# Two of four late transposes evicted on ScalarE, and one output half finished by an adding transfer

## The chip, the cores and the metric

The kernel runs on one core of one Trainium2 chip. The metric is the device time of one execution in microseconds, and the number compared is the median over several executions. Two of the core's engines matter beside TensorE (PE): VectorE (DVE) and ScalarE (ACT), which both read what PE leaves in PSUM and write SBUF. GpSimd (POOL) computes small reciprocal roots and issues the adding transfers, SyncE (SP) issues all the other transfers.

## The reference, cut to what matters

One layer of a decoder trunk, over a prompt of 1024 positions and 8 single samples, all in float32 with D = 1024:

```
xn   = rmsnorm(x, pre_g)
u, v, z_a, x_b, z_b, g_a, g_b = split(xn @ w_in)            # seven blocks of 1024 columns
y_a  = gelu(u) * spatial_mix(layernorm(gelu(v))) * silu(z_a)
y_b  = pooled(x_b) * silu(z_b)
m    = sigmoid(g_a) * (y_a @ w_pa) + sigmoid(g_b) * (y_b @ w_pb)
h    = x + rmsnorm(m @ w_out, post_g)
gate = sigmoid(rmsnorm(h, ple_in_g) @ w_pg)
y    = h + rmsnorm(gate * (p @ w_ple), ple_out_g)           # the main output
```

The change touches the start (xn is transposed, so that features lie on partitions) and the last line (the sum with h, for one half of one tile of 128 positions).

## The kernel before, in words

Tokens are cut into 8 tiles of 128 (`t` = 0 to 7) and the 8 samples (`t` = S). Every large product is one level of Strassen: seven half-size products P1 to P7. Each half-size product is three passes over the high and low parts of its operands (a float32r copy from ACT, the remainder from DVE; `split`, line 432).

**The order of the work** is not that of the code. All operations are first recorded, then a planner (class `Planner`, line 100) runs a list schedule over them with costs of its own, and writes out one fixed order for each engine. It computes for each operation a due time backwards from its readers (`late`, line 249), lets an operation start only a fixed lead ahead of that (14.98 us for a load that takes a fresh slot, 14.0 us for others; line 291), and among those that could start now takes the one with the earliest due time (line 305). It is written for `SLOTS` = 46 buffers in SBUF and for PSUM regions that it hands on in turn: three two-bank regions ("acc") and two single banks ("bank"). On the chip each engine and each queue runs its list in order and waits on semaphores.

**The start.** `begin` (line 1729) loads x, normalises it and transposes it on PE. `x_half(j, kps)` (line 965) does one half of the tokens: for each pair `kp` of feature blocks it transposes four x tiles into a PSUM region (`kp` 0, 2, 3) or two banks (`kp` 1), eight transposes in all, and evicts the pair with two instructions of 128x512 that also multiply by the norm's gain. `SIDES[4 * j + kp]` (lines 29 and 979) says by which engine: 1 is ACT, 0 is DVE. The first half (`j` = 0) is done early. The second (`j` = 1, "late") comes after the first four products, in the order of `SCRIPT` (line 36): `kp` 0 and 1, then 2 and 3, then the cut of its blocks into high and low parts.

**The end.** The last product group works on tiles 6 and 7, with its seven products in the order `LAST` (line 1622): P4 closes the first half of tile 7, P3 the second half of tile 6, and P3 is run in two column parts of 256 (`run_halves`, line 779). For each part that is ready, `gated` (line 1566) takes the sigmoid on ACT, multiplies by e on DVE, sums the squares on ACT and multiplies by the output gain on DVE. `gate_finish(t)` (line 1575) then takes the reciprocal root of the sum (one small add on DVE, one power on POOL). Tiles 0 to 5 then multiply by root and gain and have h added by a transfer of POOL that reads h from DRAM and adds it into SBUF, after which SP writes the tile out. Tiles 6, 7 and the samples load h into a slot `hback` ahead of time, and for each half of 512 columns one DVE instruction does gate times root plus h, and SP writes the half out.

Of the kernel before, what the change touches and what calls it, by code (L numbers as in the profile page):

```python
# [11 lines left out]
AF = mybir.ActivationFunctionType  # L12
ALU = mybir.AluOpType
# [3 lines left out]
NB = D // P  # L17
# [3 lines left out]
HALF = 512  # L21
# [4 lines left out]
EPS = 1e-6  # L26
POOL_BUF = 15
FAST = (1, 1, 0, 1)
SIDES = (0, 1, 0, 0, 0, 1, 0, 0)
EARLY = 40.0  # L30
WE = 1
PUSH = {'hs': -4.0, 'norm': -5.0, 'half': 0.0, 'cut': -1.0, 'e': 2.0, 'we': -2.0, 'vw': -9.0, 'p': 3.0}
# [349 lines left out]
def hybrid_step(  # L382
# [7 lines left out]
    nc = tc.nc  # L390
# [15 lines left out]
    def slot(name, shape=(P, T), dt=F32):  # L406
        n_name[0] += 1
        name, n = f"{name}_{n_name[0]}", 1
        for d in shape[1:]:
            n *= d  # L410
        model = big.rearrange("p b t -> p (b t)")[:, :n].bitcast(dt)
        if len(shape) > 2:
            dims = "abc"[: len(shape) - 1]
            model = model.rearrange(f"p ({' '.join(dims)}) -> p {' '.join(dims)}", **dict(zip(dims, shape[1:])))
        return plan.slot(name, model, lambda i: spool.tile(list(shape), dt, tag=f"slot{i}", name=name, bufs=1))
# [21 lines left out]
    def dma(out, in_, by=None):  # L437
        (by or nc.sync).dma_start(out=out, in_=in_)
# [20 lines left out]
    nc = plan  # L459
# [13 lines left out]
    def rstd(parts, n=P, r=None):  # L473

        t, r = sm("ms"), sm("rstd") if r is None else r
        nc.vector.tensor_scalar(out=t[:n], in0=parts[-1][:n], scalar1=EPS if len(parts) == 1 else parts[0][:n],
                                scalar2=None, op0=ALU.add)
        nc.gpsimd.tensor_tensor(out=r[:n], in0=t[:n], in1=mhalf[:n], op=ALU.pow)
        return r
# [312 lines left out]
    class User:  # L792

        func = AF.Copy
# [170 lines left out]
    def x_half(j, kps):  # L965

        for kp in kps:
# [9 lines left out]
            for kk in range(2):  # L977
                o, i, gain = out[:, kk], ps[kk], col(0, 2 * kp + kk)
                if SIDES[4 * j + kp]:
                    nc.scalar.activation(out=o, in_=i, func=AF.Copy, scale=gain)  # L980
# [36 lines left out]
    class V(User):  # L1017

        func = AF.Gelu_apprx_tanh
# [158 lines left out]
    class Gate(User):  # L1178
        func = AF.Sigmoid
# [7 lines left out]
    class U(User):  # L1187
        func = AF.Gelu_apprx_tanh
# [4 lines left out]
    class ZA(User):  # L1193
        func = AF.Silu
# [84 lines left out]
    class ZB(User):  # L1279
        func = AF.Silu  # L1280
# [174 lines left out]
    y_of = lambda t: y_sample if t == S else y_prompt[t * P : (t + 1) * P, :]  # L1455
# [119 lines left out]
    def gate_finish(t):  # L1575
        r = rows(t)
        rs = rstd(parts.pop(t), r)
        g = ge.pop(t)
        del e_of[t]
        if t < NB - 2:  # L1580
            nc.vector.scalar_tensor_tensor(out=g, in0=g, scalar=rs, in1=gains["out"],
                                           op0=ALU.mult, op1=ALU.mult)
            nc.gpsimd.dma_start(out=g, in_=kept["h"][t * P : (t + 1) * P, :], accum_op=ALU.add)
            dma(y_of(t), g)
            return
        h = slot("hback", (P, D))
        dma(h[:r], kept["h"][t * P : t * P + r, :])
        for j in range(2):
            nc.vector.scalar_tensor_tensor(out=g[:r, half(j)], in0=g[:r, half(j)], scalar=rs[:r],
                                           in1=h[:r, half(j)], op0=ALU.mult, op1=ALU.add)  # L1590
            dma(y_of(t)[:, half(j)], g[:r, half(j)])

    class Embed(User):
# [7 lines left out]
        def summed(self, m, j, ps, u, free=None):  # L1601
            t = 2 * self.pair + m
            o = ge[t][:, half(j)]
            add(o, ps, u)
            gated(t, half(j), o)
            if j == 0:
                gate_finish(t)
        def finish(self):
            for m in range(2):
                if 2 * self.pair + m in ge:  # L1610
                    gate_finish(2 * self.pair + m)

    def embed_gate_sample(ps):
        ge_start(S)
        o = slot("sgate", (P, D))
        sample_sums(ps, o)
        for j in range(2):
            gated(S, half(j), o[:NS, half(j)])
        gate_finish(S)
# [242 lines left out]
```

## Time and profile before

| | |
|---|---|
| median of three runs | 978.81 us (977.58 to 979.65) |
| the profiled execution's own time | 977.26 us |
| its span, first to last instruction | 975.6 us |
| PE busy | 963.1 us (99%) |
| DVE busy | 813.4 us (83%) |
| ACT busy | 497.9 us (51%) |
| POOL busy | 74.2 us (8%) |
| granted TensorE clock, mean over the span | 0.998 |

The profiled execution is one execution; 1.7 us of its time lie outside its span. It ran 1.55 us below the median of the three timed runs.

### The profile page before, as it was taken

Reading aid. Unit: us, or ns where it says so; the run is one execution under the profiler, and the core shown is the slowest. Engines: PE = TensorE matmul, PEld = TensorE weight load, DVE = VectorE, ACT = ScalarE, POOL = GpSimd, SP = SyncE. Lnnn points to the kernel's source line nnn. Section 1 sums busy time; section 2 is a strip of 40 time slices with the busy share of each in tenths; the row PEclk is TensorE's granted clock in tenths of the full one; section 3 lists DMA queues with packets and bytes.
Section 4 is the critical chain, followed back from the end, with each engine's and each line's share of the span. In section 5 each row is a group of like instructions: output and inputs, shape, how many; then the busy total and the mean of one; then the engine's idle time right before and its main releaser. Section 6 shows DMA issues by size and latency. Waiting matters only on the chain. (4 is left out here: it accounts for less than half of the span.)

```text
span 975.6 us, 15918 instructions
## 1 busy us (share of the span) xinstructions
PE 963.1 (99%) x6037; PEld 855.9 (88%) x6037; DVE 813.4 (83%) x1261; ACT 497.9 (51%) x852; POOL 74.2 (8%) x117
## 2 busy tenths in 40 slices
PE   8999999999999999999999999999999999999996
PEld 6789899999999999999999999999999997788775
DVE  6998568988889788868698897698699899779987
ACT  7664345766444443242434343563263274698655
POOL 2200000000000000000010100000000001323212
PEclk9999999999999999999999999999999999999999
DMA  9523955423467464453425366692492385799896
GB/s 327 172 105 68 192 124 183 155 97 119 164 226 261 136 203 160 140 195 120 152 99 183 134 214 238 228 384 89 158 382 92 111 301 189 151 299 313 224 320 215
DMA packets 128506, 185.82 MB, mean 190 GB/s; under 512 B 42150, under 2 KB 85198, under 8 KB 128421
## 3 DMA queue, kind: packets, MB, share of 16 engines
q1 hardware_dynamic: 126381, 177.43, 54.9%
q0 software_dynamic: 2048, 7.37, 4.1%
q8 instruction: 47, 0.77, 0.3%
q14 instruction: 30, 0.25, 0.1%
HBM read 129.27 MB, written 55.96 MB: 190 GB/s over the span
## 5 line engine op out<-in xcount | busy, mean ns | idle before, releaser
L374 DVE TENSOR_TENSOR u<-acc,u 128x520 f32<-128x520 f32 (+1 forms) x89 | 62.0, 696 | 35.5 <-PE acc L374 35.2
L374 POOL TENSOR_TENSOR rstd<-ms,mhalf 128x1 f32<-128x1 f32 (+1 forms) x37 | 30.9, 841 | 520.3 <-DVE ms L374 517.7
L374 ACT ACTIVATE u<-acc 128x512 f32<-128x512 f32 (+1 forms) x43 | 25.6, 596 | 44.2 <-PE acc L374 44.0
L374 DVE TENSOR_TENSOR big<-big 128x1024 f32<-128x1024 f32 (+4 forms) x20 | 23.8, 1219 | 0.0
L374 POOL COPY big<-xb 128x1 f32<-128x1 f32 x8 | 3.4, 419 | 260.4 <-ACT xb L374 219.7
L374 ACT ACTIVATE paw<-pas 128x512 fp32r<-128x512 f32 x16 | 10.0, 630 | 24.0 <-DVE pas L374 18.2
L374 ACT ACTIVATE pbw<-pbs 128x512 fp32r<-128x512 f32 x16 | 10.0, 628 | 22.1 <-DVE pbs L374 16.8
L374 PE MATMUL accm<-qh,wpoolw 128*128 128x260 f32 (+1 forms) x96 | 20.9, 319 | 0.0
L374 ACT ACTIVATE big<-mix 128x256 f32<-128x256 f32 x32 | 12.0, 382 | 17.1 <-PE mix L374 16.4
L374 ACT ACTIVATE gbw<-gbs 128x512 fp32r<-128x512 f32 x16 | 10.1, 630 | 19.3 <-DVE gbs L374 10.0
L374 DVE SCALAR_TENSOR_TENSOR zb<-accm,gvec,zb 128x512 f32<-128x512 f32 (+1 forms) x16 | 12.0, 754 | 9.4 <-PE accm L374 9.2
L374 ACT ACTIVATE zaw<-zas 128x512 fp32r<-128x512 f32 x16 | 10.0, 628 | 18.1 <-DVE zas L374 10.0
L374 ACT ACTIVATE junk<-h 128x512 bf16<-128x512 f32 x25 | 15.7, 628 | 3.4 <-DVE h L374 2.9
L374 PEld LDWEIGHTS accm<-qh,wpoolw 128*128 128x128 f32 x96 | 15.6, 188 | 1.9
L374 ACT ACTIVATE zbw<-zbs 128x512 fp32r<-128x512 f32 x16 | 10.1, 628 | 13.8 <-DVE zbs L374 8.2
L374 ACT ACTIVATE u<-acct 128x512 f32<-128x512 f32 x22 | 13.0, 589 | 7.4 <-PE acct L374 4.6
L374 DVE TENSOR_TENSOR paw<-pas,paw 128x512 fp32r<-128x512 f32 x16 | 10.9, 688 | 6.7 <-ACT paw L374 6.7
L374 ACT ACTIVATE mw<-ms 128x512 fp32r<-128x512 f32 x16 | 10.0, 625 | 12.4 <-DVE ms L374 9.7
L374 ACT ACT_TABLE_LOAD x11 | 14.1, 1283 | 4.0 <-PE acc L374 2.3
L374 ACT ACTIVATE zbw<-zbraw 128x512 fp32r<-128x512 f32 x12 | 7.5, 623 | 16.6 <-DMA zbraw<-in_w_in_dram 10.7
L374 ACT ACTIVATE gbw<-gbraw 128x512 fp32r<-128x512 f32 x12 | 7.4, 624 | 16.4 <-DMA gbraw<-in_w_in_dram 14.3
L374 PE MATMUL mix<-wst,vh 128*128 128x256 f32 x64 | 15.5, 320 | 0.0
(655 smaller groups left out, 3560.5 us busy)
## 6 DMA issues: line engine op xcount, KB each, us to landing
ga<-ga SPq DMA_DIRECT2D x16, 516.0 KB, 4.6
gb<-gb SPq DMA_DIRECT2D x16, 516.0 KB, 6.2
ya<-za SPq DMA_DIRECT2D x8, 516.0 KB, 3.6
yb<-zb SPq DMA_DIRECT2D x8, 516.0 KB, 4.5
x<-in_x_prompt_dram SPq DMA_DIRECT2D x8, 512.0 KB, 9.3
vraw<-in_w_in_dram SPq DMA_DIRECT2D x8, 512.0 KB, 6.4
e<-e SPq DMA_DIRECT2D x8, 512.0 KB, 3.6
vturned<-v SPq DMA_DIRECT2D x32, 128.0 KB, 4.5
```

What stands on the lines that cost most here:

```text
L374: getattr(getattr(self.nc, e), method)(*(self.real(a) for a in args), **{k: self.real(a) for k, a in kwargs.items()})
```

## The change

Two edits. The table `SIDES` gives the late pairs `kp` 0 and 2 to ACT, where before it gave `kp` 1 alone; `kp` 1 goes back to DVE. And for tile 6 (the seventh) the second half is finished otherwise: SP copies the second half of h from its slot to the output; ACT multiplies the gate by the root in place; POOL issues a transfer from SBUF to the output in DRAM that adds. The first half of tile 6, tile 7 and the samples stay as they were.

```diff
-SIDES = (0, 1, 0, 0, 0, 1, 0, 0)
+SIDES = (0, 1, 0, 0, 1, 0, 1, 0)
...
         h = slot("hback", (P, D))
         dma(h[:r], kept["h"][t * P : t * P + r, :])
+        if t == NB - 2:
+            dma(y_of(t)[:, HALF:], h[:, HALF:])
         for j in range(2):
+            if t == NB - 2 and j:
+                nc.scalar.activation(out=g[:, HALF:], in_=g[:, HALF:], func=AF.Copy, scale=rs)
+                nc.gpsimd.dma_start(out=y_of(t)[:, HALF:], in_=g[:, HALF:], accum_op=ALU.add)
+                continue
             nc.vector.scalar_tensor_tensor(out=g[:r, half(j)], in0=g[:r, half(j)], scalar=rs[:r],
                                            in1=h[:r, half(j)], op0=ALU.mult, op1=ALU.add)
             dma(y_of(t)[:, half(j)], g[:r, half(j)])
```

## Rows read from the trace of the kernel before

**Rows 1.** The page: span, and busy time of the two busiest engines.

```profile
span 975.6 us, 15918 instructions
PE 963.1 (99%) x6037; PEld 855.9 (88%) x6037; DVE 813.4 (83%) x1261; ACT 497.9 (51%) x852; POOL 74.2 (8%) x117
```

**Rows 2.** Busy time by stage: us, then each engine; clock, transfers' share, GB/s.

```profile
41.00:911.00 870.00, 870.00 (x5582) 784.43 (x5582) 728.50 (x1110) 430.11 (x718) 47.77 (x56) 1.00 0.56 180
...
967.60:975.60 8.00, 0.00 (x0) 0.00 (x0) 4.51 (x10) 1.36 (x5) 1.53 (x2) 0.72 0.59 231
```

**Rows 3.** PE in order of time around the late transposes; idle time in brackets.

```profile
35.96 2.78 PE L374 MATMUL pst<-ident,x 128*128 128x128 f32 x24
39.46 1.06 PE L374 MATMUL pst<-ident,x 128*128 128x128 f32 x8 [0.72 <-DVE big L374]
40.78 0.47 PE L374 MATMUL acc<-xB11h,vw 128*128 128x512 f32 x1 [0.25 <-DVE big L374]
```

**Rows 4.** PE in order of time, the last part of P3.

```profile
966.20 0.39 PE L374 MATMUL acct<-wgB22h,hw 128*128 128x256 f32 x1 [0.56 <-ACT ge L374]
```

**Rows 5.** DVE in order of time in the same stretch as rows 3.

```profile
37.91 4.07 DVE L374 TENSOR_SCALAR big<-pst,gvec 128x512 f32<-128x512 f32 x6 [0.21 <-PE pst L374]
```

**Rows 6.** ACT in order of time in the same stretch.

```profile
37.73 0.63 ACT L374 ACTIVATE vw<-vs 128x512 fp32r<-128x512 f32 x1 [0.97 <-DVE vs L374]
38.27 1.25 ACT L374 ACTIVATE big<-pst,gvec 128x512 f32<-128x512 f32 x2
40.67 1.07 ACT L374 ACTIVATE xB22h<-big 128x1040 fp32r<-128x1040 f32 x1 [1.15 <-DVE big L374]
```

**Rows 7.** POOL in order of time: the last reciprocal root, tile 6's.

```profile
969.89 0.66 POOL L374 TENSOR_TENSOR rstd<-ms,mhalf 128x1 f32<-128x1 f32 x1 [1.43 <-DVE ms L374]
```

**Rows 8.** DVE in order of time: its last two instructions, tile 6's two halves.

```profile
970.73 1.41 DVE L374 SCALAR_TENSOR_TENSOR ge<-ge,rstd,hback 128x512 f32<-128x512 f32 x2
```

**Rows 9.** ACT in order of time: an instruction of 128x512 on SBUF.

```profile
966.49 0.63 ACT L374 ACTIVATE junk<-ge 128x512 bf16<-128x512 f32 x1 [0.34 <-DVE ge L374]
```

**Rows 10.** SP in order of time: the issues of tile 6's two halves.

```profile
971.50 0.33 SPq L374 DMA_DIRECT2D out_dram<-ge  x1
972.16 0.33 SPq L374 DMA_DIRECT2D out_dram<-ge  x1
```

**Rows 11.** The tile out_dram from 969 on: issue to landing of the last outputs.

```profile
L374 SPq DMA_DIRECT2D out_dram<-ge x4: 332/332/333, 969.7 to 972.2; - x4
...
DMA to landing us min/median/max: 2.1/2.1/2.1
```

**Rows 12.** The tile h, 903 to 905: one adding transfer, 512 KB, DRAM to SBUF.

```profile
L374 POOL DMA_DIRECT2D h<-in_x_prompt_dram x1: 879/879/879, 904.0 to 904.0; - x1
...
DMA to landing us min/median/max: 5.3/5.3/5.3
```

**Rows 13.** The tile ge, 955 to 957.2: the last but one adding transfer, 512 KB.

```profile
L374 POOL DMA_DIRECT2D ge<-h x1: 894/894/894, 956.5 to 956.5; - x1
...
DMA to landing us min/median/max: 5.7/5.7/5.7
```

**Rows 14.** Transfer queues: packets, MB, share of 16 engines; 959 to 961, then 970.4 to 971.3.

```profile
q0 software_dynamic: 92, 0.38, 95.1%
...
q1 hardware_dynamic: 139, 0.26, 76.1%
```

**Rows 15.** The tile hback: its loads, and issue to landing of the last.

```profile
L374 SPq DMA_DIRECT2D hback<-h x3: 291/319/492, 948.4 to 958.7; - x3
...
DMA to landing us min/median/max: 9.6/9.6/9.6
```

**Rows 16.** Busy time by stage near the end, columns as in rows 2.

```profile
962.00:966.00 4.00, 3.64 (x24) 3.08 (x22) 4.00 (x9) 2.25 (x6) 0.15 (x1) 1.00 1.00 275
966.00:969.50 3.50, 1.34 (x9) 1.14 (x9) 2.96 (x8) 2.25 (x8) 0.93 (x1) 1.00 1.00 403
969.50:972.00 2.50, 0.00 (x0) 0.00 (x0) 2.50 (x6) 0.00 (x0) 0.66 (x1) 0.81 0.45 175
```

## The prediction

> **What bounds the kernel now.** I read the busy totals first: PE is busy for 963.1 of 975.6 us, DVE for 813.4 and ACT for half [rows 1]. A total is an average, so next the table by stage: from 41 to 911 us PE is busy for 870.00 of 870.00 us [rows 2]. No edit to DVE or ACT work in that stretch can shorten it; it could only open a hole in it. What PE loses lies at the two ends. So I went to PE in order of time and looked for its brackets. Around the late transposes it stands still twice, 0.72 us before the last pair is transposed and 0.25 us before the next product, both times because DVE has not yet emptied PSUM [rows 3]; near the end it waits 0.56 us for ACT between the two parts of P3 [rows 4]. Last, the stage behind PE's last instruction: 8.0 us from 967.6 to the end in which PE does nothing and the time is a chain of small steps [rows 2]. Both edits lie in these places: the first can touch the 0.72 and 0.25 us, the second the last 8 us. Together they can't give much, and the question is the sign.
>
> **Part 1, the late transposes.** Before, DVE empties pairs 0, 2 and 3, six instructions in 4.07 us (0.68 us from one to the next), beginning when PE has transposed the last x tile at 37.91 us [rows 5]; ACT empties pair 1, two in 1.25 us (0.62 each) [rows 6]. Pair 3 needs the region of pair 0, and PE restarts at 39.46, which is 37.91 + two DVE instructions + a handover of about 0.15 us [rows 3, 5]. The product at 40.78 waits for the region of pair 2, the fourth DVE instruction [rows 3, 5].
>
> After, ACT has pairs 0 and 2, DVE pairs 1 and 3. No instruction is added or removed, two change places: DVE loses 1.36 us of work in a stage where it is the late one, ACT gains 1.25 us in one where it idled 1.15 us straight afterwards [rows 6]. ACT is free when pair 0 is ready, if the weight split that stands at 37.73 [rows 6] goes behind the evictions. It should: the planner ranks by due time, and pair 0's region is wanted by the next transposes at once, while that split feeds a later product. Then: ACT takes pair 0 at 37.91 and is through at 39.16 (1.25 us), PE restarts at about 39.31 instead of 39.46; pair 3's transposes (1.06 us) end at 40.37; ACT takes pair 2 from 39.16 to 40.41, so the product can start near 40.50 instead of 40.78. Gain about 0.3 us, and since PE is solid from there to 911 us [rows 2], it is carried to the end of PE's work. The bounds: if the split stays in front, ACT starts pair 0 at 38.27 [rows 6], and the restart comes at 39.67, 0.2 us later than before; if both holes closed, 0.97 us would be won [rows 3], which the transposes of pair 3 in series with an eviction don't allow. I take −0.3. What hides the rest: the cut of the second half, 1.07 us on ACT at 40.67 [rows 6], begins when pair 2 is out, and that comes no later than before.
>
> **Part 2, the end.** Before, tile 6's root leaves POOL at 969.89 + 0.66 = 970.55 [rows 7]. DVE is still busy with tile 7 and does tile 6's halves as its last two instructions from 970.73 to 972.14 [rows 8]. SP issues them at 971.50 and 972.16 [rows 10], and 2.1 us after the last issue the transfer has landed [rows 11]: 974.26. The remaining 1.3 us of the span is the program's close and stays.
>
> Removed: one DVE instruction (0.70 us, half of rows 8) and the last SP issue. With nothing in their place the last landing would be that of the first half, 971.50 + 2.1 = 973.6, a gain of 0.65 us.
>
> Added, on the path: ACT's product, 0.63 us by an instruction of the same size [rows 9], from 970.6, when the root is there, to 971.25 (ACT has little else there: 1.36 us of work in those last 8 us [rows 2]). Then POOL issues the adding transfer at about 971.3. Nothing is queued behind it on POOL. That is 0.86 us ahead of the old last issue. But the transfer is of another kind. The trace has adding transfers of 512 KB alone, from DRAM into SBUF: 5.3 us from issue to landing [rows 12], 5.7 us with a second one beside it [rows 13]. None of 256 KB and none into DRAM is shown. In the stretch with only the adding queue at work, 92 packets of 4 KB took 95.1% of 16 engines for 2.0 us, so 0.33 us each [rows 14]; 128 rows over 16 engines are 8 packets in turn, 2.65 us. Rows half as long, at the same rate per byte, save 1.3 us: 5.3 − 1.3 = 4.0 us. Bounds: 2.1 us if it is no dearer than a plain write of the same bytes [rows 11], 5.7 us if the cost goes by packets and not by bytes [rows 13]. I take 4.0, since it is made of the nearest rows. Landing 971.3 + 4.0 = 975.3, against 974.26 before: +1.05 us. With the bounds, from 973.6 (the first half is then last, −0.65) to 977.0 (+2.75).
>
> The Trainium skill, page "DMA: Bandwidth & Descriptors", section "Anatomy of one DMA — SWDGE (gpsimd) path", fits such a transfer as about 2.0 us plus bytes over 436 thousand per us, so an estimate of 2.6 us for 256 KB and 3.2 us for 512 KB. By it the transfer would land at 973.9, 0.35 us ahead of before, and the median would be some 978.2 us. For 512 KB this trace shows 5.3 us [rows 12] and not 3.2, so here the measurement decides.
>
> Added, off the path: SP copies the second half of h to the output, one issue of about 0.33 us [rows 10] and 256 KB. By rows 14 a plain 256 KB (some 128 packets of 2 KB at 76.1% of 16 engines in 0.9 us) is about 0.7 us of all engines. It falls into a stage in which the engines are full, 1.00 from 962 to 969.5 [rows 16], and pushes the outputs of tiles 4 and 5 back by 0.7 us; from 969.5 to 972 the share is 0.45 [rows 16], which takes that up before the last transfers. It adds two waits. SP waits for the load of h before it can issue the copy, and behind it in SP's order stand the samples' and the tiles' outputs; POOL waits for the copy's landing. The last load of h takes 9.6 us from its issue at 958.7, until 968.3 [rows 15], because the adding transfers hold the engines. I expect the load to move up, as it now has a reader with an earlier due time (the planner adds issue and transfer of the copy, some 3 us against 0.8 us for the DVE instruction), so the copy is out before 968 and this costs nothing. If the cover fails, it is the second rival.
>
> **The sum.** −0.3 + 1.05 = +0.75 us on the profiled execution: 977.26 to 978.0. That execution was 1.55 us below the median of the runs shown, so the forecast for the median is 978.81 + 0.8 = 979.6 us. What a measurement of this kernel can tell from no change is 0.2%, here 1.96 us: 976.85 to 980.77.
>
> **Rivals.**
> 1. *The adding transfer costs by the packet.* For: there are 128 rows either way, and an adding packet of 4 KB took 0.33 us, four times the 0.08 us of a plain one of 2 KB (76.1% of 16 engines, 0.9 us, 139 packets), so more than bytes is in it [rows 14]. Against: the plain 2 KB packets are so short that a floor per packet is not in sight. It decides if a 2 KB adding packet takes as long as the 0.33 us of a 4 KB one. Then 5.7 us, landing 977.0: +2.75 − 0.3 = +2.45, 981.3 us, slower.
> 2. *The copy of h blocks SP.* If the planner leaves the load where it is and puts the copy ahead of the outputs, SP stands until 968.3. Then 256 KB of h, two outputs of 512 KB, three of 256 KB and the adding transfer of 1.3 us follow in one stream: 0.7 + 2 × 1.3 + 3 × 0.7 + 1.3 = 6.7 us from the first packet at about 969.1, so 975.8, and with some 0.2 us to the landing 976.0: +1.75 − 0.3, 980.3 us. For: the 9.6 us [rows 15]; against: the earlier due time.
> 3. *The adding transfer is cheap.* If it is hardly dearer than a plain write of the same bytes, 2.1 to 2.5 us, it lands by 973.8 and the end is that of DVE's half or just behind: −0.45 to −0.65, with −0.3: 978.0 us. For: the engines are not full by then [rows 16]. Against: 5.3 us in rows 12. The Trainium skill's fit above is of this kind.
> 4. *The new order opens a hole in the middle.* All planned work behind 38 us is put in order anew, with other buffers. For: 870 us without a hole [rows 2] leave only one direction. Against: ACT is busy for half of that stretch, DVE for 84%, so there is slack. 1.5 to 3 us: 982 us.
> 5. *The first edit does nothing*, as the order on ACT keeps the split in front: +0.2 instead of −0.3, 980.1 us.
>
> **How the numbers follow.** Forecast (978.9 to 980.4) 47%, rival 1 16%, rival 2 8%, rival 3 16%, rival 4 6%, rival 5 7%. The range holds 8 in 10 if it reaches from rival 3 to rival 1 with the scatter of a median (the three runs lie within 2 us): 977.6 to 981.7. Slower by over 0.2%: most of rival 1, rival 4, and the upper edge of rival 2: 0.20. Faster by over 0.2% needs 1.96 us, but the holes and the gain at the end add up to 0.97 + 0.65 = 1.6 us at the very best: 0.04, for scatter. Within: 0.76.
>
> **What would show it.** In the profile after: PE's brackets at 39 to 41 us sum to about 0.65 us instead of 0.97; ACT has four evictions of 128x512 there, ahead of the split; PE's last instruction comes about 0.3 us earlier; DVE ends with one instruction for tile 6; an ACT instruction of 0.63 us follows POOL's root, and POOL's issue comes near 971 us; its landing is 4.0 us later and ends the span. Wrong would be: an adding transfer of under 3 us or over 5, SP idle from 963 to 968 us ahead of the copy, or a bracket of PE between 41 and 911 us.

## The result, and the profile after

The changed kernel takes 980.28 us (median of 17 runs, 978.52 to 984.65), the kernel before 978.84 us (17 runs, 976.88 to 980.66): ratio over all runs 1.0020, 95% interval [1.0012, 1.0028], so 1.2 to 2.7 us slower (the two medians alone give 1.0015). The forecast was 0.8 us slower, 979.6. The profiled execution of after took 981.77 us, with a span of 980.1; it lies 1.5 us above its median, and that of before 1.55 us below its own, so of the 4.5 us between the two spans a good part is not the change.

First the page of after, to be held against [rows 1]:

```profile
span 980.1 us, 15910 instructions
PE 965.2 (98%) x6037; PEld 856.7 (87%) x6037; DVE 811.0 (83%) x1258; ACT 499.7 (51%) x855; POOL 75.4 (8%) x118
```

PE is busy for 2.1 us longer with the same 6037 matmuls. That hints that something beside waits has changed, but it is only a hint: run 2 below, in which PE's pace is that of before, also has 964.9 us. Next PE in order of time around the late transposes, against [rows 3] (start, duration, operation, idle time in brackets):

```profile
36.51 3.44 PE L374 MATMUL pst<-ident,x 128*128 128x128 f32 x30
39.77 1.18 PE L374 MATMUL acc<-xB11h,vw 128*128 128x512 f32 x4
40.80 0.38 PE L374 MATMUL pst<-ident,x 128*128 128x128 f32 x2
40.93 0.71 PE L374 MATMUL acc<-xB11l,vw 128*128 128x512 f32 x2
...
42.41 0.39 PE L374 MATMUL e<-wehi,ph 128*128 128x512 f32 x1
```

No bracket is left: both holes are gone, 30 of the 32 transposes follow one another, and four matmuls of the next product go ahead of the last two. The last of these rows is the first product with the next weights; in the trace of before, in the same view, it is

```profile
43.18 0.39 PE L374 MATMUL e<-wehi,ph 128*128 128x512 f32 x1
```

The same stretch on ACT, against [rows 6]:

```profile
36.71 0.60 ACT L374 ACTIVATE v<-acc 128x512 f32<-128x512 f32 x1 [1.25 <-PE acc L374]
38.45 2.42 ACT L374 ACTIVATE big<-pst,gvec 128x512 f32<-128x512 f32 x4 [1.15 <-PE pst L374]
40.91 1.07 ACT L374 ACTIVATE xB22h<-big 128x1040 fp32r<-128x1040 f32 x1
41.89 1.14 ACT L374 ACTIVATE vw<-vs 128x512 fp32r<-128x512 f32 x2
```

and on DVE, against [rows 5]:

```profile
38.56 1.41 DVE L374 TENSOR_SCALAR big<-pst,gvec 128x512 f32<-128x512 f32 x2 [0.34 <-PE pst L374]
39.89 0.68 DVE L374 TENSOR_TENSOR vs<-vraw,vraw 128x512 f32<-128x512 f32 x1
40.60 0.69 DVE L374 TENSOR_TENSOR vs<-vs,vraw 128x512 f32<-128x512 f32 x1
41.21 1.41 DVE L374 TENSOR_SCALAR big<-pst,gvec 128x512 f32<-128x512 f32 x2
```

The product before the transposes is emptied first (`v<-acc`), then come four evictions on ACT, the weight split behind them, and two pairs of instructions on DVE with room between. Then what PE waited for in the rest of the span; the view's columns are who waits for whom, us in total, times and the longest:

```profile
PE acct L374 <- ACT ge L374: 1.0, 1, 1.0
PE acct L374 <- ACT u L374: 1.0, 2, 0.5
```

The first is the wait inside P3, 0.56 us before [rows 4] and 0.6 in every run below, so the 1.0 is this execution's own; the second, two waits at 873 and 893 us, is not in the trace of before. Last the end, against [rows 7 to 11]: POOL, ACT and DVE in order of time, then the last two issues and the time from issue to landing (least, median, most).

```profile
972.78 0.66 POOL L374 TENSOR_TENSOR rstd<-ms,mhalf 128x1 f32<-128x1 f32 x1 [1.25 <-DVE ms L374]
974.61 0.92 POOL L374 DMA_DIRECT2D out_dram<-ge  x1 [1.17 <-ACT ge L374]
```

```profile
973.48 0.72 ACT L374 ACTIVATE ge<-ge,rstd 128x512 f32<-128x512 f32 x1 [1.39 <-POOL rstd L374]
```

```profile
972.95 1.41 DVE L374 SCALAR_TENSOR_TENSOR ge<-ge,rstd,hback 128x512 f32<-128x512 f32 x2
```

```profile
L374 SPq DMA_DIRECT2D out_dram<-ge x1: 333/333/333, 974.4 to 974.4; - x1
L374 POOL DMA_DIRECT2D out_dram<-ge x1: 923/923/923, 974.6 to 974.6; - x1
...
DMA to landing us min/median/max: 2.2/3.1/4.1
```

The root is out at 972.78 + 0.66 = 973.44; ACT is through at 974.20; POOL issues 0.41 us later, at 974.61; and of the two transfers SP's plain one takes 2.2 us and POOL's adding one 4.1, so the adding one ends the work at 974.61 + 4.1 = 978.7. From the root to that landing it is 5.3 us; before it was 974.26 − 970.55 = 3.7 [rows 7, 10, 11].

### The profile page after: what moved, and what is told of

The parts are those of the page before. It is cut to its first block, busy times and chain, and to the rows that moved or that the text cites. A ratio compares the mean times of both kernels' runs of the same rounds, so it can differ in the third digit from the quotient of the medians.

```text
span 980.1 us, 15910 instructions
## 1 busy us (share of the span) xinstructions
PE 965.2 (98%) x6037; PEld 856.7 (87%) x6037; DVE 811.0 (83%) x1258; ACT 499.7 (51%) x855; POOL 75.4 (8%) x118
## 5 line engine op out<-in xcount | busy, mean ns | idle before, releaser
L374 ACT ACTIVATE uw<-us 128x512 fp32r<-128x512 f32 x16 | 10.0, 626 | 12.5 <-DVE us L374 11.0
```

Of the source, the lines that this page charges most:

```text
L374: getattr(getattr(self.nc, e), method)(*(self.real(a) for a in args), **{k: self.real(a) for k, a in kwargs.items()})
```

## The experiments

Twelve kernels were run. The first four share a chip and one set of runs of before, the next four another, then three and one; each ratio is against its own set.

**1. The first edit alone.**

```diff
-SIDES = (0, 1, 0, 0, 0, 1, 0, 0)
+SIDES = (0, 1, 0, 0, 1, 0, 1, 0)
```

> The first edit alone; the end is as before. Theory (the loss is the adding transfer at the end, the first edit wins a little): PE's two brackets of 0.72 and 0.25 us at 39 to 41 us are gone, PE's last instruction comes 0.5 to 1.3 us earlier than in the kernel before, root to last landing stays 3.7 us, and the median is 0.3 to 1.3 us below before (ratio 0.9987 to 0.9997). Rival (the new order of all planned work costs something between 41 us and the end): PE's end no earlier, brackets of PE at 870 to 900 us as in the kernel after, median 0 to 1 us above before.

Measured: 978.75 us, ratio 0.9999 [0.9990, 1.0008]. Both holes at 39 to 41 us are closed as in after, yet the time is that of before. The gain is made and lost again. Neither expectation held whole: the median isn't below before, and of the rival's brackets at 870 to 900 us there is one, of 0.26 us.

**2. The second edit alone** (`SIDES` as before, the six added lines of `gate_finish` kept).

> The second edit alone; the late transposes are as before. Theory: root to last landing 5.2 us as in the kernel after instead of 3.7, PE's brackets at 39 to 41 us stay 0.97 us, median 1.5 to 2.0 us above before (ratio 1.0015 to 1.002). Rival (the new order costs): root to landing still 5.2, but the median is no more than 1.0 us above before, with the rest of the loss of 1.4 us coming with the first edit.

Measured: 980.27 us, ratio 1.0018 [1.0010, 1.0027]: the whole loss. POOL in order of time, and the landings from 971.4 us on:

```profile
971.47 0.66 POOL L374 TENSOR_TENSOR rstd<-ms,mhalf 128x1 f32<-128x1 f32 x1 [1.43 <-DVE ms L374]
973.29 0.92 POOL L374 DMA_DIRECT2D out_dram<-ge  x1 [1.16 <-ACT ge L374]
```

```profile
DMA to landing us min/median/max: 2.0/3.0/3.9
```

From the root (972.13) to the landing (973.29 + 3.9 = 977.2) it is 5.1 us.

**3. After, with POOL's last transfer a plain write** (that half is then without h).

```diff
-                nc.gpsimd.dma_start(out=y_of(t)[:, HALF:], in_=g[:, HALF:], accum_op=ALU.add)
+                nc.gpsimd.dma_start(out=y_of(t)[:, HALF:], in_=g[:, HALF:])
```

> The kernel after, but POOL's last transfer writes instead of adding, so h is left out of the second half of tile 6. It prices the adding by itself: same queue, same bytes, same waits. Theory (the adding is dear): issue to landing falls from 4.07 us to about 2.6 us, the median by about 1.3 us against the kernel after, to within 0.3 us of before. Rival (what is dear is a transfer from POOL's queue, whatever it does): issue to landing stays above 3.6 us and the median changes by under 0.5 us.

Measured: 978.33 us, ratio 1.0000 [0.9991, 1.0009]. The same engine, queue, bytes and place, and only the adding gone:

```profile
L374 SPq DMA_DIRECT2D out_dram<-ge x1: 333/333/333, 971.4 to 971.4; - x1
L374 POOL DMA_DIRECT2D out_dram<-ge x1: 622/622/622, 971.6 to 971.6; - x1
...
DMA to landing us min/median/max: 2.2/2.4/2.6
```

2.6 us instead of 4.1: the loss at the end is the adding. A part of it is in POOL's own issue, which took 0.62 us here and 0.92 in after (the 622 and 923 ns of the rows).

**4. After, with SP writing that half, plain** (again without h).

```diff
-                nc.gpsimd.dma_start(out=y_of(t)[:, HALF:], in_=g[:, HALF:], accum_op=ALU.add)
+                dma(y_of(t)[:, HALF:], g[:, HALF:])
```

> The kernel after, but the scaled second half of tile 6 is written by SP without adding, so h is left out there too. It prices POOL's issue and queue: against e3 only the queue differs. Theory: issue to landing 2.1 us, and the last landing is then that of DVE's first half or of this one, about 2.0 us before that of the kernel after; the median 1.5 to 2.3 us below after, 0.2 to 0.8 us below before. Rival (POOL's queue costs nothing beside SP's, the adding is all): the median within 0.3 us of e3.

Measured: 978.12 us, ratio 1.0001 [0.9992, 1.0010]. Against run 3 that is 0.2 us, which these runs can't resolve: whose queue it is costs nothing that shows. The 2.1 us from issue to landing did not come: in the trace SP's write issued at 971.88, when ACT was through, landed 2.9 us later, 3.7 us behind the root, as POOL's did in run 3.

**Where the early gain goes.** PE has no bracket from 71 to 855 us in these traces, but for one of 0.2 us in run 3, at a granted clock of 1.00, so the place to look is the time that PE takes between two fixed products. In order of time on PE, the first product of an early and of a late group, in before:

```profile
70.61 0.40 PE L374 MATMUL acc<-xT1h,vw 128*128 128x260 f32 x2
...
855.01 0.39 PE L374 MATMUL acct<-woB21h,mw 128*128 128x512 f32 x1
```

and in after:

```profile
69.92 0.40 PE L374 MATMUL acc<-xT1h,vw 128*128 128x260 f32 x2
...
855.55 0.39 PE L374 MATMUL acct<-woB21h,mw 128*128 128x512 f32 x1
```

784.40 us before, 785.63 after: the same matmuls take 1.23 us longer, in the same order but for two groups of 24 that change places at 80 to 86 us. The view by stage shows PE busy for all 784.00 us from 71 to 855 in both, at a clock of 1.00. Its counts, 5156 matmuls and 5148, are no measure of the pace: PE comes to 71 us at another place in its work, and run 5 below, which isn't slow, has 5150.

```profile
71.00:855.00 784.00, 784.00 (x5156) 713.72 (x5155) 648.77 (x995) 362.86 (x602) 30.32 (x41) 1.00 0.55 176
```

```profile
71.00:855.00 784.00, 784.00 (x5148) 713.17 (x5147) 646.50 (x992) 362.61 (x601) 30.08 (x41) 1.00 0.55 176
```

In runs 1, 3 and 4, all with the new `SIDES`, the stretch takes 785.44, 785.86 and 785.41 us; in run 2, with the old one, 784.45. So it goes with the first edit, and not with the chip, which these four runs share. What that edit changes behind 42 us, beside the order on DVE and ACT and the two groups on PE, is which tensors go into which PSUM region and which of the 46 slots. A slot is as long as the longest tensor that it holds, 4160 bytes per partition in nearly all and 4128 in one before, and they lie one behind another; a slot of 4128 moves the start of all later ones by 32 bytes against a multiple of 64. In the layout before, 4 slots begin at a multiple of 64 and 42 lie 32 past one; after, 25 and 21, since a second slot is now short. That gave a theory that could be tried without touching the order of the work.

**5. The first edit, all slots 4160 bytes long.** The slots' tensors become views of one size, here and in 6, 7 and 9 to 12; 46 slots begin at a multiple of 64. In the built programs every engine does the same in the same order as in run 1, with the same slots and PSUM regions; only the addresses in SBUF differ. The same holds for 6, 7, 9 and 10 against before, and for 11 against after.

```diff
-        return plan.slot(name, model, lambda i: spool.tile(list(shape), dt, tag=f"slot{i}", name=name, bufs=1))
+        def make(i):
+            t = spool.tile([P, 1040], F32, tag=f"slot{i}", name=name, bufs=1)[:, :n].bitcast(dt)
...
+        return plan.slot(name, model, make)
```

> The first edit alone, with every slot in SBUF 4160 bytes long, so that all slots begin at a multiple of 64 bytes; nothing in the order of the work changes against the first edit alone. Theory (PE runs slower when its operands lie in slots of which some begin at 0 and some at 32 bytes past a multiple of 64): PE keeps the 1.35 us that it is ahead at 42 us, so PE ends 0.9 to 1.5 us earlier than before, and the ratio is 0.9986 to 0.9992. Rival (the steady loss comes from the new order, or from which buffers are handed to whom): PE loses 1.0 to 1.2 us between 71 and 870 us again, and the ratio is 0.9995 to 1.0005.

Measured: 977.25 us, ratio 0.9993 [0.9984, 1.0003]. By the time alone the two theories aren't told apart (the interval holds both), but the trace does it: the stretch takes 784.26 us, and the gain is still there at 855 us.

**6. Before, all slots 4160 bytes long.**

> The kernel before, with every slot 4160 bytes long, so that all begin at a multiple of 64 bytes (before, nearly all begin 32 bytes past one). Same order. Both theories: within 0.5 us of before, ratio 0.9995 to 1.0005; the theory of the starts needs in addition that PE, measured from 42 to 870 us, takes the same time as before within 0.2 us. If PE is faster than before by over 0.5 us there, a start at a multiple of 64 is better in itself, and not only a mixture worse.

Measured: 977.13 us, ratio 0.9997 [0.9989, 1.0006]. PE in order of time:

```profile
70.79 0.40 PE L374 MATMUL acc<-xT1h,vw 128*128 128x260 f32 x2
...
854.79 0.39 PE L374 MATMUL acct<-woB21h,mw 128*128 128x512 f32 x1
```

784.00 us, 0.4 us shorter than before, a little outside what the theory allowed.

**7. Before, with the mixture put in by hand**: 21 slots at a multiple of 64, 25 at 32 past one, same order and same slots for the same tensors as in 6 (the edit is shown against 6).

```diff
-            t = spool.tile([P, 1040], F32, tag=f"slot{i}", name=name, bufs=1)[:, :n].bitcast(dt)
+            t = spool.tile([P, 1048 if i == MID else 1040], F32, tag=f"slot{i}", name=name, bufs=1)[:, :n].bitcast(dt)
```

with `MID = 20`.

> The kernel before, with the slots of the first part beginning at a multiple of 64 bytes and those behind the twentieth 32 bytes past one. Same order. Theory (mixed starts slow PE): PE takes 0.5 to 1.2 us longer than before between 71 and 870 us, spread evenly and without a bracket; ratio 1.0005 to 1.0012. Rival (the new order or the hand-out of buffers): PE takes the same time as before within 0.2 us there, ratio 0.9995 to 1.0005.

Measured: 978.80 us, ratio 1.0013 [1.0002, 1.0024]. PE in order of time (line 375 here is line 374 elsewhere):

```profile
70.55 0.41 PE L375 MATMUL acc<-xT1h,vw 128*128 128x260 f32 x2
...
856.46 0.40 PE L375 MATMUL acct<-woB21h,mw 128*128 128x512 f32 x1
```

785.91 us: 1.9 us longer than run 6, on the same chip, for 32 bytes put in once, and slower than before by the ratio too. Against before it is 1.5 us, a little more than the 0.5 to 1.2 expected.

**8. After, with the adding transfer cut to 256 columns**, to see what the adding costs by.

```diff
-                nc.gpsimd.dma_start(out=y_of(t)[:, HALF:], in_=g[:, HALF:], accum_op=ALU.add)
+                nc.gpsimd.dma_start(out=y_of(t)[:, HALF + 256 :], in_=g[:, HALF + 256 :], accum_op=ALU.add)
```

> The changed kernel, with POOL's adding transfer cut to the last 256 of its 512 columns (rows of 1 KB, 128 KB in all; the 256 columns between are left with h alone). Theory (an adding transfer costs by the byte: 5.3 us for 512 KB, 4.07 us for 256 KB, so some 1.2 us less again for half): 2.9 to 3.5 us from issue to landing. Rival (it costs by the packet, 128 rows either way): 3.9 to 4.2 us.

Measured: one execution of 977.57 us, and the landing:

```profile
L374 POOL DMA_DIRECT2D out_dram<-ge x1: 926/926/926, 971.5 to 971.5; - x1
...
DMA to landing us min/median/max: 2.2/2.6/3.0
```

3.0 us for 128 KB against 3.7 to 4.1 for 256 KB (after, runs 2 and 11), with 128 rows each time: what changes goes by the bytes and not by the rows. By estimate about 2 us don't go by the bytes, among them POOL's issue, 0.93 us here and 0.92 in after.

**9 and 10. Two controls on run 7**: the same inserted place with 64 bytes instead of 32 (`1056 if i == MID`; all 46 slots stay at a multiple of 64), and 32 bytes so late that 2 slots and the small buffers behind them move (`MID = 24`).

> The kernel before, with slots of 4160 bytes, and the twentieth 64 bytes longer instead of 32: everything behind it moves, but all slots still begin at a multiple of 64 bytes. Theory (it is the mixture of starts at 0 and 32 past a multiple of 64 that slows PE): PE takes as long as before from 71 to 870 us, within 0.4 us; ratio 0.9993 to 1.0005. Rival (the place of the buffers counts, not the start's remainder): PE 0.8 us or more slower there, as with the 32 bytes; ratio 1.0006 to 1.0015.

> The kernel before, with slots of 4160 bytes, and 32 bytes put in so late that only the last two of the 46 slots, and the small buffers behind them, begin 32 bytes past a multiple of 64. Theory (the mixture among the slots): only a small part of the pairs of operands is mixed, so PE is at most 0.3 us slower than before from 71 to 870 us; ratio 0.9993 to 1.0006. Rival (what counts is the small buffers behind the slots): PE 0.8 us or more slower there; ratio 1.0006 to 1.0015.

Measured: 976.82 us, 0.9991 [0.9982, 1.0000], stretch 783.61 us; and 977.60 us, 0.9998 [0.9989, 1.0007], stretch 784.33. So neither moving the buffers nor moving the small ones behind them slows PE. The 64 bytes even made the stretch 0.8 us shorter than before, where 0.4 was the most expected, and 0.4 us shorter than run 6; so place counts in some other way too, which no run here explains.

**11. After, all slots 4160 bytes long.**

> The changed kernel, with every slot 4160 bytes long, so that all begin at a multiple of 64 bytes; same order as the changed kernel. Theory: PE keeps the 1.3 us or so that it is ahead at 42 us, apart from brackets behind 860 us; with the adding transfer's 1.6 us at the end the ratio to before is 1.0000 to 1.0012, some 1 us below the changed kernel. Rival (the order or the hand-out of buffers takes the time): ratio 1.0010 to 1.0025, as the changed kernel.

Measured: 978.12 us, ratio 1.0004 [0.9995, 1.0013]. The stretch:

```profile
69.64 0.40 PE L374 MATMUL acc<-xT1h,vw 128*128 128x260 f32 x2
...
853.90 0.39 PE L374 MATMUL acct<-woB21h,mw 128*128 128x512 f32 x1
```

784.26 us. With the change's own work untouched, even slots bring the ratio from 1.0020 to 1.0004 (the two intervals overlap by 0.0001): PE keeps its early gain, and what stands against it is the adding, 3.7 us to the landing in this run. From its first late transpose to the late product above PE takes 819.05 us before, 819.04 after (gained and lost), and 817.61 here and in run 5.

**12. The best of these**: the first edit, slots as in 9, the end as before.

> The first edit alone (two late pairs on ACT), with slots of 4160 bytes and the twentieth 64 bytes longer, so that all slots begin at a multiple of 64 bytes; the end of the kernel as before. Theory (the gain at 42 us is kept where no starts are mixed, and the 0.8 us that the 64 bytes brought from 71 to 855 us come again): 1.4 + 0.8 us ahead of before, ratio 0.9973 to 0.9988. Rival (those 0.8 us belonged to that one order and hand-out of buffers): only the early gain, ratio 0.9984 to 1.0000, as for the first edit with slots of 4160 bytes.

Measured: 976.73 us, ratio 0.9990 [0.9981, 0.9999]; stretch 783.92 us. By its interval it is 0.1 to 1.9 us ahead of the kernel before, and so ahead of the changed one. The interval reaches into both expectations, and run 9, which lacks the edit, has nearly the same ratio; so how much of the gain is the edit's is not told by the times. In the traces PE takes 817.24 us from its first late transpose to the late product, against 818.24 in run 9 and 819.05 before, one execution each: 1.0 us of 1.8 goes with the edit. Of run 9's 0.8 us in the stretch 0.5 came again.

The stretch in all, against the starts of the slots:

| kernel | slots at 0 / at 32 past 64 | first to last product, us | against before |
|---|---|---|---|
| before; run 2 | 4 / 42 | 784.40; 784.45 | 0; +0.05 |
| after; runs 1, 3, 4, 8 | 25 / 21 | 785.63; 785.44, 785.86, 785.41, 785.41 | +1.0 to +1.5 |
| run 7 | 21 / 25 | 785.91 | +1.5 |
| runs 5, 6, 9, 11, 12 | 46 / 0 | 784.26, 784.00, 783.61, 784.26, 783.92 | −0.8 to −0.1 |
| run 10 | 44 / 2 | 784.33 | −0.1 |

Each is one execution, but the two kinds don't overlap, and both occur on each of the two chips that ran runs 1 to 8: the six traces with about half of the slots on either start lie at 785.4 and above, the eight others at 784.45 and below.

## Why the prediction was right or wrong

Right in its sign, and about half of the size: +0.75 us was forecast and 1.2 to 2.7 measured. That part 1 came near its forecast is luck, for two errors of about 1 us each cancel in it; the size was missed in part 2.

**Part 1, right about ACT, wrong in two steps.** ACT did take its four evictions ahead of the weight split, as argued from the due times, and DVE was no longer the late one. But the gain at the place was not 0.3 us. From the first late transpose to the next product with `wehi` PE took 43.18 − 35.96 = 7.22 us before and 42.41 − 36.51 = 5.90 after: 1.3 us, more than the 0.97 us of the two brackets, which the prediction had called out of reach.

The first step that failed is "Pair 3 needs the region of pair 0", true of before and carried over to after, and with it "the transposes of pair 3 in series with an eviction don't allow". In after 30 transposes start 0.109 us apart (36.51 to 39.77), so pair 3's first starts at about 39.13, while ACT is still emptying pair 0, until about 39.66 (38.45 and half of 2.42). They go elsewhere: the built program gives pair 3 the region of the product before the transposes, which ACT had emptied by 37.31 (`v<-acc`), and the next product that of pair 0, which can so start at 39.77, 0.11 us behind pair 0's eviction.

A bracket is also not the whole price of a hole, as it begins only where the last matmul before it ends. By the same 0.109 us, 24 transposes take 2.61 us from start to start and 8 take 0.87; before, PE took 39.46 − 35.96 = 3.50 and 40.78 − 39.46 = 1.32. The holes cost 0.89 + 0.45 = 1.3 us, and that is what was won.

Then the second step failed, "since PE is solid from there to 911 us, it is carried to the end". Without a bracket PE still lost 1.23 us of it. The runs show that the pace goes with the starts of the slots (7 against 6, 9 and 10; 5 against 1; 11 against after). Part 1 is thus −1.3 + 1.2, near 0 as in run 1 (−0.1 us, give or take 0.9), where −0.3 was forecast. Nor did PE end 0.3 us earlier: the last part of P3 starts at 966.20 us before [rows 4], at 968.83 in after and at 965.98 to 966.77 in runs 1, 3, 4 and 8.

**Part 2, right in kind, mis-sized in two of three terms.** The adding transfer: forecast 4.0 us to the landing, worked out by the byte from rows of 512 KB; measured 4.1, 3.9 and 3.7, and run 8 bears out the way by the byte. ACT's product: forecast 0.63 us, measured 0.72. The row it came from multiplies by no column [rows 9], this one by a column of 128x1 in SBUF, the root. It isn't the type that it writes: a split into float32r without a column takes 0.63 as well [rows 6], and the trace of before had the nearer row, `ge<-ge,hscales`, with a column, eight of 128x512 at 0.72 us on average. Of 128x1024 into float32r, `vh<-big,npart` takes 1.15 us there and `vh<-big`, without the column, 1.06. ACT to POOL's issue: forecast as good as none (971.25 to "about 971.3"), measured 0.41. POOL's root to the product was 0.04 us. Root to landing grew by 5.3 − 3.7 = 1.6 us (in run 2 by 1.4), where +1.05 was forecast.

**The copy of h** cost nothing, as forecast. SP on either side of it, in order of time in after:

```profile
966.30 0.30 SPq L374 DMA_DIRECT2D out_dram<-ge  x1
966.70 0.34 SPq L374 DMA_DIRECT2D out_dram<-hback  x1
```

SP goes from the samples' output to the copy without standing still (it had stood until 966.30, for DVE's product of the samples and not for the load of h), and POOL's issue, 7.9 us after the copy's, waits last for ACT and not for the copy; runs 3 and 4 hold it and are no slower than before. DVE ends with one instruction for tile 6, as said. The split of sums: −0.1 for part 1 and +1.6 for part 2 give +1.5 us, inside the measured 1.2 to 2.7. Run 2, which has part 2 alone, is 1.0 to 2.6 us slower by its interval.

**The rivals.**

1. By the packet: out, by run 8 and by the 3.7 to 4.1 us where it had 5.7.
2. SP blocked: out, by the rows above.
3. Hardly dearer than a plain write: out by run 3, 2.6 us plain against 4.1 adding. This is also where the Trainium skill, page "DMA: Bandwidth & Descriptors", section "Anatomy of one DMA — SWDGE (gpsimd) path", can be placed: its fit for a transfer of POOL's, an estimate of 2.6 us for 256 KB, agrees with the 2.6 us of run 3; for the adding kind, 3.7 to 4.1 us here, it doesn't hold, and the prediction was right to let the rows decide.
4. A hole between 41 and 911 us: of the kind that was meant, two brackets of 0.55 and 0.43 us appear in the profiled execution of after, and 0.47 and 0.39 in run 2. By the prediction's own list that is a sign of being wrong. But runs 4, 8 and 11, with the same order on PE, have none, and run 9, with the order of before on every engine, has one of 0.47 at 891 us; so they come and go, they aren't owed to the new order alone, and their part in the median stays open. What the rival missed is that PE can lose time there with no hole at all.
5. The first edit does nothing: right in its result (run 1), wrong in its way.

What stays open: which access is slowed by the mixture. That 32 bytes make the difference is shown, by runs 6 and 7, which differ in nothing else; whether it is PE's loads of weights against its stream, or PE against another engine, no run here tells.

## What to carry to other kernels

An adding transfer at the end of a kernel is paid in full: here it cost 1.1 to 1.5 us over a plain write of the same 256 KB, while the DVE instruction that it replaced took 0.7. A hole is priced from start to start of the matmuls around it, since its bracket understates it: here 1.3 us against 0.97. Before a gain is carried through a stretch "without a hole", compare the times of two fixed instructions at its ends: a busy share of 100% doesn't say that the pace is the same. And where an edit changes what is put into which buffer, look at the addresses on both sides, or keep all buffers of one length; otherwise the layout becomes a second change that no line of the diff shows.

## What the runs showed of the hardware

PE's pace depended on where the buffers in SBUF begin. With slots of which some begin at a multiple of 64 bytes and about half 32 past one, 784 us of PE work without a bracket took 1.0 to 1.5 us longer than before, and up to 2.3 us longer than with all at a multiple of 64 (785.91 against 783.61). The Trainium skill, page "SBUF — State Buffer", section "SBUF: two separate sides", says that PE's port never waits on another engine; no run here shows whether this slowing contradicts it, since it may lie within PE's own two reads.

An adding transfer from SBUF into DRAM took 3.0 us for 128 KB and 3.7 to 4.1 us for 256 KB, so by estimate about 1 us for each 128 KB on top of some 2 us; a plain one by the same queue took 2.6 us for 256 KB. POOL's issue alone took 0.92 us adding 256 KB, 0.93 adding 128, and 0.62 us plain. The time from the end of ACT's product to POOL's issue was 0.41 us in after.

An ACT instruction of 128x512 that also reads a column of 128x1 from SBUF took 0.72 us, one without it 0.63. Matmuls that follow one another overlapped in the trace: 30 transposes of 128x128 started 0.109 us apart, and eight of them took 1.06 us from the first start to the last end, where 8 × 0.109 is 0.87.
